# Rotating images by 180 degrees: SyncE's first load waits for a small memset on GpSimd

## The chip, the cores and the metric

The kernel runs on one core of one Trainium2 chip. The metric is the device time of one execution in microseconds (us). The kernel before took 122.02 us in the median of four runs (121.86 to 122.14).

## The reference

The input holds 32 x 3 images of 256 x 256 float32 numbers, 25.17 MB. The output has the same shape: each image turned by 180 degrees, which means that the 65,536 numbers of an image are written in reverse order.

```python
def reference(x):                       # x: (32, 3, 256, 256) float32
    return np.rot90(x, k=2, axes=(-2, -1)).astype(np.float32)
```

## The kernel before

The 96 images are taken in three groups of 32. In each group an image is cut into four rows of E = 16,384 numbers (64 KB), so a group is a tile of 128 partitions x 64 KB, which holds 8.39 MB. The tiles `A`, `Bt` and `Ct` hold the three groups, each in a buffer of its own, and all three groups stay in the on-chip memory: no load ever waits for a buffer. `T` is a scratch tile of 128 x 2,048 numbers (J = E / 8).

The work on one group has three steps.

- `load` brings rows from DRAM to a tile, in the order in which they stand there. One row of a load is one DMA packet for each partition.
- `inside` reverses the numbers of every row in place, on VectorE (DVE): for each of four pairs of blocks of 2,048 numbers it copies the upper block reversed to `T`, the lower block reversed to the upper place, and `T` to the lower place. These are 12 copies for each tile (line 52).
- `store` writes the tile back with the four rows of each image in reverse order (line 58). The reversal of the row order costs no instruction; it is in the address pattern.

Some transfers are cut in two. The load of `A` has a strip of the first `HEAD` = 512 numbers (2 KB of each row, 256 KB in all), issued by ScalarE (ACT); the other 62 KB of each row come in a second load, issued by SyncE (SP). The load of `Ct` is cut at its last 1,536 numbers (`TAIL`, 6 KB of each row). The store of `A` is cut after its first 128 numbers (`LEAD`, 512 bytes of each row). All transfers other than the strip are issued by SP, in this order: the rest of `A`, `Bt`, the body of `Ct`, the tail of `Ct`, the lead of `A`'s store, the rest of `A`'s store, the store of `Bt`, the store of `Ct`. The profile shows SP's queue as q1 and ACT's queue as q10. Both queues feed the same 16 DMA engines.

Two orders are written by hand. The DVE copies are kept in program order, and the large store of `A` waits until the body of `Ct` has landed, so that the tail of `Ct` is still on its way while that store is issued. The tile framework adds the remaining waits from the data that instructions share.

In the profile, lines 55 (loads), 52 (copies) and 58 (stores) carry the work; line 100 is the launch's preamble, with four small memsets on GpSimd (POOL), and line 111 its end.

Of the kernel before, what the change touches and what calls it, by code (L numbers as in the profile page):

```python
# [2 lines left out]

os.environ.setdefault("NEURON_RT_ULTRASERVER_MODE", "4")

# [4 lines left out]


@with_exitstack
def kernel(
    ctx: ExitStack,
    tc: tile.TileContext,
    x: bass.AP,
    out: bass.AP,
):

    nc = tc.nc
    P = 128

    B, C, H, W = x.shape
    L = H * W
    G = 32
    E = L // 4
    J = E // 8

    x4 = x.rearrange("b c h w -> (b c) (h w)").rearrange(
        "(g n) (s e) -> g (n s) e", n=G, s=4)
    o4 = out.rearrange("b c h w -> (b c) (h w)").rearrange(
        "(g n) (s e) -> g n s e", n=G, s=4)  # L40

    pool = ctx.enter_context(tc.tile_pool(name="slots", bufs=1))
    A = pool.tile([P, E], x.dtype, tag="A")
    Bt = pool.tile([P, E], x.dtype, tag="B")
    Ct = pool.tile([P, E], x.dtype, tag="C")
    T = pool.tile([P, J], x.dtype, tag="T")

    def back(t, lo, hi):
        return t[:, hi - 1:(lo - 1 if lo else None):-1]

    def copy(dst, src):
        tc.keep_in_program_order(nc.vector.tensor_copy(out=dst, in_=src))  # L52

    def load(t, g, lo, hi, queue=nc.sync):
        return queue.dma_start(out=t[:, lo:hi], in_=x4[g][:, lo:hi])  # L55

    def store(t, g, lo, hi):
        return nc.sync.dma_start(
            out=o4[g][:, ::-1, lo:hi], in_=t[:, lo:hi])

    def inside(t):
        for lo in range(0, E // 2, J):
            hi = E - lo - J
            copy(T[:, :], back(t, hi, hi + J))
            copy(t[:, hi:hi + J], back(t, lo, lo + J))
            copy(t[:, lo:lo + J], T[:, :])

    TAIL = 1536
    HEAD = 512
    load(A, 0, 0, HEAD, nc.scalar)  # L70
    load(A, 0, HEAD, E)
    load(Bt, 1, 0, E)
    body = load(Ct, 2, 0, E - TAIL)
    load(Ct, 2, E - TAIL, E)
    inside(A)
    LEAD = 128
    store(A, 0, 0, LEAD)
    first = store(A, 0, LEAD, E)
    tc.add_manual_dep(
        first.ins, body.ins.name,  # L80
        mybir.DependencyInfo(mybir.DependencyClass.Sync, mybir.DependencyReason.DATA),
        reason="the first store is queued while the last strip is on its way")
    for g, t in ((1, Bt), (2, Ct)):
        inside(t)
        store(t, g, 0, E)


# [1 line left out]
_INS = ['x']  # L89
_OUTS = [((32, 3, 256, 256), 'float32')]  # L90


# [23 lines left out]
```

## Time and profile before

| quantity | value |
|---|---|
| median of 4 runs | 122.02 us (121.86 to 122.14) |
| profiled execution, device time | 121.99 us |
| its span, first to last instruction | 120.2 us |
| DVE busy | 44.2 us (37%), 36 copies of 1.23 us |
| POOL busy | 0.2 us, 4 memsets of about 0.1 us |
| DMA, share of 16 engines | q1 97.0%, q10 0.6% |
| bytes | 25.17 MB read, 25.17 MB written, 419 GB/s over the span |
| issue of `A`'s rest (SP) and strip (ACT) | both at 0.73 us |
| landing after issue | rest 22.0 us, strip 22.1 us |

How to read it: the span is counted from the first instruction to the last; the device time of the profiled execution is 1.79 us longer. In a view by stretches of time, a DMA packet is counted whole, with its bytes and its duration, in the stretch in which it starts. So a short stretch in which 16 large packets start shows a DMA share far above 1, and the next stretch shows zero although the engines are at work. GB/s times the length of the stretch gives the bytes of the packets that started there, and the DMA share times the length times 16 gives the sum of their durations.

### The profile page before, as it was taken

What the parts mean: (1) busy time and instruction counts of PE and PEld (TensorE: products, weight loads), DVE (VectorE), ACT (ScalarE), POOL (GpSimd) and SP (SyncE); (2) the same over time, 40 slices, a digit from 0 to 9 for tenths busy, and PEclk for the clock granted to TensorE, in tenths of its full rate; (3) what the DMA queues carried; (4) which work ended last, traced back from release to release, by engine and by line L of the source; (5) the groups of instructions that cost most, each with busy time, mean ns of one, the idle gap of its engine ahead of it and who ended that gap; (6) DMA issues with size and microseconds to landing.
All of it is one profiled execution on the core that took longest, in us unless ns stands there. A gap on an engine that the chain in (4) does not pass through costs nothing.

```text
span 120.2 us, 97 instructions
## 1 busy us (share of the span) xinstructions
DVE 44.2 (37%) x36; POOL 0.2 (0%) x4
## 2 busy tenths in 40 slices
DVE  0000000499995099999049999500000000000000
POOL 0000000000000000000000000000000000000000
DMA  9888988898889779779499777988898889888990
GB/s 338 349 349 371 655 370 349 360 676 371 349 349 676 338 316 613 336 316 632 192 438 692 346 346 346 692 349 349 349 698 349 349 349 676 371 349 349 654 393 0
DMA packets 1296, 50.33 MB, mean 419 GB/s; under 512 B 144, under 2 KB 272, under 8 KB 528
## 3 DMA queue, kind: packets, MB, share of 16 engines
q1 hardware_dynamic: 1152, 50.07, 97.0%
q10 hardware_dynamic: 144, 0.26, 0.6%
HBM read 25.17 MB, written 25.17 MB: 419 GB/s over the span
## 4 chain that ended last, share of the span: by engine, by line
DMA 34%; DVE 25%; another core or an unknown queue 3%; issue 1%; SPq 0%; DVEq 0%
DMA Bt<-in_x_dram 34%; DVE T L52 8%; DVE Ct L52 8%; DVE Bt L52 8%; SPq L55 0%; DVEq L52 0%
## 5 line engine op out<-in xcount | busy, mean ns | idle before, releaser
L52 DVE COPY T<-A 128x2048 f32<-128x2048 f32 x4 | 4.9, 1227 | 22.8 <-DMA A<-in_x_dram 22.7
L52 DVE COPY T<-Bt 128x2048 f32<-128x2048 f32 x4 | 4.9, 1227 | 4.4 <-DMA Bt<-in_x_dram 4.3
L52 DVE COPY T<-Ct 128x2048 f32<-128x2048 f32 x4 | 4.9, 1227 | 4.4 <-DMA Ct<-in_x_dram 4.3
L52 DVE COPY A<-A 128x2048 f32<-128x2048 f32 x4 | 4.9, 1227 | 0.1
L52 DVE COPY Bt<-Bt 128x2048 f32<-128x2048 f32 x4 | 4.9, 1227 | 0.1
L52 DVE COPY Ct<-T 128x2048 f32<-128x2048 f32 x4 | 4.9, 1227 | 0.1
L52 DVE COPY Ct<-Ct 128x2048 f32<-128x2048 f32 x4 | 4.9, 1226 | 0.1
L52 DVE COPY A<-T 128x2048 f32<-128x2048 f32 x4 | 4.9, 1226 | 0.1
L52 DVE COPY Bt<-T 128x2048 f32<-128x2048 f32 x4 | 4.9, 1226 | 0.1
L100 POOL MEMSET const-bfloat16-1.0<- 128x1 bf16 x1 | 0.1, 102 | 0.0
L100 POOL MEMSET const-uint8-127<- 128x1 uint8 x1 | 0.1, 101 | 0.0
L100 POOL MEMSET const-float32-0.0<- 128x1 f32 x1 | 0.1, 99 | 0.2 <-issue 0.2
L100 POOL MEMSET const-float32-1.0<- 128x1 f32 x1 | 0.1, 98 | 0.0
## 6 DMA issues: line engine op xcount, KB each, us to landing
out_dram<-A SPq DMA_DIRECT2D x1, 8128.0 KB, 21.2
A<-in_x_dram SPq DMA_DIRECT2D x1, 7936.0 KB, 22.0
Ct<-in_x_dram SPq DMA_DIRECT2D x1, 7424.0 KB, 57.9
Ct<-in_x_dram SPq DMA_DIRECT2D x1, 768.0 KB, 59.3
A<-in_x_dram ACTq DMA_DIRECT2D x1, 256.0 KB, 22.1
out_dram<-A SPq DMA_DIRECT2D x1, 64.0 KB, 35.2
Bt<-in_x_dram SPq DMA_DIRECT2D x1, 40.9
out_dram<-Bt SPq DMA_DIRECT2D x1, 39.8
```

The costliest lines, as they stand in the source:

```text
L52: tc.keep_in_program_order(nc.vector.tensor_copy(out=dst, in_=src))
L100: nc = _bacc.Bacc("TRN2", target_bir_lowering=False, num_devices=1)
```

## The change

Before the loads, GpSimd gets a memset of the first 16 numbers of each row of `T` (`pause`). SP's load of the 62 KB of each row of `A` gets a manual dependency on that memset, with a semaphore. ACT's load of the strip has no such dependency. `load` now also keeps the loads in the program's order among themselves.

```diff
     def load(t, g, lo, hi, queue=nc.sync):
-        return queue.dma_start(out=t[:, lo:hi], in_=x4[g][:, lo:hi])
+        return tc.keep_in_program_order(
+            queue.dma_start(out=t[:, lo:hi], in_=x4[g][:, lo:hi]))
...
     HEAD = 512
+    pause = nc.gpsimd.memset(T[:, :16], 0.0)
     load(A, 0, 0, HEAD, nc.scalar)
-    load(A, 0, HEAD, E)
+    rest = load(A, 0, HEAD, E)
+    tc.add_manual_dep(
+        rest.ins, pause.ins.name,
+        mybir.DependencyInfo(mybir.DependencyClass.Sync, mybir.DependencyReason.DATA),
+        reason="the long packets are queued behind the strip")
     load(Bt, 1, 0, E)
```

## Prediction

> **What bounds the kernel now.** I read the page first: engine busy times, the DMA slices and the queues.
>
> ```profile
> DVE 44.2 (37%) x36; POOL 0.2 (0%) x4
> ...
> q1 hardware_dynamic: 1152, 50.07, 97.0%
> q10 hardware_dynamic: 144, 0.26, 0.6%
> ```
>
> The 16 DMA engines are busy 97.6% of 120.2 us, and DVE 37%. The 2.4% that is left is 2.9 us, and the windows below place most of it: the first packet starts after 1.70 us, and the last ones (started at 116.4 to 116.7, about 2.42 us long) end at about 119.1. So the kernel is bound by DMA from its first packet to its last, and this change can only move when the engines start and how evenly they run. The chain of waits names DVE for 25%, but it follows copies that the queue covers: the wait at the end is SP's, for the last store.
>
> ```profile
> SPq L111 <- DMA out_dram<-Ct: 38.6, 1, 38.6
> ```
>
> The last store was issued at 76.70 us and its packets began about 20 us later, behind other stores. DVE could finish many microseconds later at no cost.
>
> Next the timeline of the first 3 us.
>
> ```profile
> 0.33 0.10 POOL L100 MEMSET const-uint8-127<- 128x1 uint8 x1
> 0.73 0.39 SPq L55 DMA_DIRECT2D A<-in_x_dram  x1
> 0.73 0.38 ACTq L55 DMA_DIRECT2D A<-in_x_dram  x1
> 1.18 0.43 SPq L55 DMA_DIRECT2D Bt<-in_x_dram  x1
> 1.65 1.00 SPq L55 DMA_DIRECT2D Ct<-in_x_dram  x2
> ```
>
> SP's large load and ACT's strip are issued in the same moment. Which goes first is seen in the windows. Their columns are the stretch, its length, DVE and POOL busy time, clock, DMA share and GB/s; a packet counts where it starts.
>
> ```profile
> 1.70:2.10 0.40, 0.00 (x0) 0.00 (x0) 1.00 7.63 2540
> 2.10:4.60 2.50, 0.00 (x0) 0.00 (x0) 1.00 0.00 0
> 4.60:4.70 0.10, 0.00 (x0) 0.00 (x0) 1.00 0.05 20
> 4.70:5.30 0.60, 0.00 (x0) 0.00 (x0) 1.00 3.79 1638
> 5.30:5.40 0.10, 0.00 (x0) 0.00 (x0) 1.00 1.46 635
> 5.40:6.90 1.50, 0.00 (x0) 0.00 (x0) 1.00 0.00 0
> 6.90:7.80 0.90, 0.00 (x0) 0.00 (x0) 1.00 2.70 1165
> ```
>
> From 1.70 to 2.10 us, 2540 GB/s x 0.40 us = 1016 KB start, which is 16 x 63.5 KB: all 16 engines begin with a long packet and none with a 2 KB one. Their durations sum to 7.63 x 0.40 x 16 = 48.8 us, **3.05 us** each. From 4.60 to 4.70 one 2 KB packet starts (20 x 0.10 = 2 KB, 0.05 x 0.10 x 16 = **0.08 us**). From 4.60 to 5.40 together, 2 + 983 + 63.5 = 1049 KB start, which is 16 short and 16 long packets; from 6.90 to 7.80 it is 1049 KB again, lasting 2.70 x 0.90 x 16 = 38.9 us. Less 16 x 0.08 this is 37.6, or **2.35 us** for a long packet. So engines alternate, one packet of each queue, and the first long packet costs 0.70 us more than the second. Its excess is not equal on all engines: the first packets start within 0.40 us at most, but the second long ones start from 4.7 up to 5.3-5.4 us, a spread of 0.6 to 0.7.
>
> The lag stays. At the turn from loads to stores, the first long store packets start mostly in one 0.1 us stretch, and one engine follows late:
>
> ```profile
> 60.90:61.00 0.10, 0.00 (x0) 0.00 (x0) 1.00 11.14 4700
> 61.00:61.10 0.10, 0.00 (x0) 0.00 (x0) 1.00 6.13 2632
> 61.10:61.20 0.10, 0.00 (x0) 0.00 (x0) 1.00 0.07 20
> 61.20:61.30 0.10, 0.00 (x0) 0.00 (x0) 1.00 1.56 666
> ```
>
> **The change part by part.** The sum is made against the profiled execution, 121.99 us (span 120.2, and 1.79 around it), 0.03 us under the median of the runs.
>
> SP's wait. POOL's preamble rows end at 0.43 us, and SP and ACT begin at 0.73, so I let POOL begin there too. Its memset is 128x16; the nearest row is the 128x1 memset, 0.10 us. No row shows a POOL semaphore releasing an SP load; the nearest is DVE's copy, which ends at 26.47 (25.24 + 1.23) and releases SP's store at 26.50, 0.03 us. So SP issues at about 0.88 instead of 0.73: 0.15 us later. The upper bound is 0.5, as if the memset took as long as the preamble's four (0.20 us busy) and 0.3 went to the wait and its instruction. The lower bound is 0.1, the memset alone. I take 0.15 to 0.2, by the nearest rows. The three loads queued behind on SP (`Bt`, both parts of `Ct`) go back by as much, and for them it costs nothing: `A`'s packets keep the engines busy until about 22 us. DVE, which waits for `A` at 22.7, does not set the end.
>
> On the DMA engines 0.15 to 0.2 us is no loss if strip packets fill it. Per engine there are 8 x 0.08 = 0.67 us of strip (256 KB over 16 engines, 2 KB each). If the strip's first packets start where the long ones did, at 1.70 to 2.10, the long packets join at about 1.9 to 2.3, and from then each engine has work of both kinds, as before. Term: 0. With the cover gone it is +0.15 to +0.5.
>
> The first packet. Bytes and packets are the same, so the strip-first order saves nothing by itself. What can change is the 0.70 us excess. If it is a fixed start cost of an engine, the first 2 KB packet bears it and the term is 0. If it comes from 16 engines starting 62 KB reads together, it shrinks with the packet, by up to 0.70 x 60/62 = 0.68. A side below nothing (small first packets start worse) is not excluded by any row, but from 1.9 us on the long packets are there to fill a stall, so I bound it at +0.3. A fixed cost would hit all engines alike; the spread grew from at most 0.40 to 0.6-0.7, so some 0.2 to 0.3 is unequal, and I read that as contention. I take **-0.3**, near the unequal part.
>
> The rest. DVE's first copy gets one more wait, on a memset finished 21 us earlier: 0. SP's closing waits may get one more semaphore: 0 to +0.05, taken as 0. Program order among the loads is the order that they had: 0. POOL's extra memset has no one behind it but the end.
>
> Sum: 121.99 + 0 - 0.3 = 121.69, so **121.7 us**.
>
> The Trainium skill, "DMA: Bandwidth & Descriptors", section "Issuing engines are not separate DMA queues", speaks against a gain: transfers from different engines run on the same 16 DMA engines and a second issuer saves only issue time. The trace agrees that one set of engines serves both queues (they alternate above); by that rule alone the order is worth nothing and the time would be 122.0.
>
> The same page, section "Queues, rings and completion order", says that an engine drains a whole packet of typically 9 to 17 descriptors before it changes the queue. The rows above show a change after every single row of 2 KB. By the rule all eight strip rows of an engine would go in one turn; the sum is the same by both, since the engines stay busy.
>
> **The rivals.** *A wash, 122.0.* The excess is a fixed start cost and goes to the first 2 KB packet, and the wait hides behind the strip. For it: the bytes are unchanged, and the lag of the slowest engine shrinks by itself, from about 0.3 us behind most others at 61.2-61.3 to about 0.1 at the last packets (4588 GB/s in each of the stretches 116.4 to 116.5 and 116.5 to 116.6 is 459 KB, 7 packets of 64 KB each; the other two start from 116.6 to 116.7). Against it: the unequal excess. 0 to +0.2 gives 122.0 to 122.2.
>
> *The strip still isn't first, 122.3.* Both loads were issued at 0.73, yet all 16 engines took SP's packet first. If ACT's queue reaches the engines later by more than SP's new delay, the long packets go first again and everything starts later by the wait, with nothing in front. Place: the stretch from 1.7 to 2.1 us. Price: +0.15 to +0.5, 122.15 to 122.5, in the middle 122.3. It decides if ACT's first packets come over 0.2 us later than SP's did. No row excludes that, because ACT's packets had the long ones in front of them from 2.1 us. For it: 16 of 16 engines agree. Against: the two issues began and ended within 0.01 us of each other, so a small lead of SP's is enough to explain the order.
>
> **How the numbers follow.** About 0.2%, 0.24 us, is what a measurement of this kernel can tell from no change. Strip first with a smaller excess (121.7): 0.45. Wash (122.0): 0.27. Strip not first, or small packets that start worse (122.3): 0.28. The forecast's own range is 121.3 (excess gone) to 121.9; its weak end is a change within 0.2%, some 0.05 of its chance, and a long wait in the wash gives the slow side 0.02. So faster 0.40, same 0.30, slower 0.30. The range: 121.3 to 122.5 holds the cases; I set 121.25, for the runs' spread of 0.14 on either side, to 122.5.
>
> **What would show it.** Right: the timeline has SP's issue at 0.85 to 0.95 and ACT's at 0.73; the window 1.70 to 2.10 starts 2 KB packets; the strip lands earlier than the 22.1 us after its issue of now, and at most 0.2 us later than now the rest of `A`; the slowest engine's first long store packet starts before 61.2. Wrong: long packets of about 3.05 us still first, 0.2 us later; or the short first packets with an excess of 0.7 each, and the turn to the stores where it is now; or engines idle between the strip and the first long packet.

## The result and the profile after

The changed kernel takes 122.20 us in the median of 31 runs (122.01 to 122.58), the kernel before 122.02 us in 50 runs beside it. The ratio is 1.0016 (95% interval 1.001 to 1.0021): slower by 0.18 us, where -0.3 us was forecast. The profiled execution took 122.14 us with a span of 120.3 us, against 121.99 and 120.2 before.

The change does what it says. The timeline of the changed kernel from 0.6 us on (start, length, engine, line, operation):

```profile
0.73 0.11 POOL L71 MEMSET T<- 128x16 f32 x1 [0.29 <-POOLq L106]
0.73 0.36 ACTq L56 DMA_DIRECT2D A<-in_x_dram  x1
0.87 0.38 SPq L56 DMA_DIRECT2D A<-in_x_dram  x1
```

SP's large load is issued at 0.87 us in place of 0.73, 0.14 us later, and ACT's strip still at 0.73. The page of the changed kernel has the queues and, in its last column, the time from issue to landing:

```profile
q1 hardware_dynamic: 1152, 50.07, 96.5%
q10 hardware_dynamic: 144, 0.26, 0.9%
...
A<-in_x_dram SPq DMA_DIRECT2D x1, 7936.0 KB, 21.8
...
A<-in_x_dram ACTq DMA_DIRECT2D x1, 256.0 KB, 2.9
```

The strip lands 2.9 us after its issue, where it was 22.1 before: it goes first. The rest of `A` lands at 0.87 + 21.8 = 22.7 us, and before it was 0.73 + 22.0 = 22.7. So at the end of the first load nothing is won and nothing lost. The waits of DVE say the same for all three tiles (in total, times, longest):

```profile
DVE T L52 <- DMA A<-in_x_dram: 22.7, 1, 22.7
DVE T L52 <- DMA Ct<-in_x_dram: 4.3, 1, 4.3
DVE T L52 <- DMA Bt<-in_x_dram: 4.2, 1, 4.2
```

The kernel before had

```profile
DVE T L52 <- DMA A<-in_x_dram: 22.7, 1, 22.7
DVE T L52 <- DMA Bt<-in_x_dram: 4.3, 1, 4.3
DVE T L52 <- DMA Ct<-in_x_dram: 4.3, 1, 4.3
```

Where the start cost went is in the windows of the changed kernel (stretch, length, DVE, POOL, clock, DMA share, GB/s):

```profile
1.70:3.40 1.70, 0.00 (x0) 0.00 (x0) 1.00 2.06 752
3.40:5.05 1.65, 0.00 (x0) 0.00 (x0) 1.00 0.00 0
5.05:5.85 0.80, 0.00 (x0) 0.00 (x0) 1.00 2.95 1270
```

A KB is 1,000 bytes in these products. From 1.70 to 3.40 us, 752 x 1.70 = 1278 KB start: all 128 strip packets (262 KB) and the first long packet of each engine (1016 KB). Their durations are 2.06 x 1.70 x 16 = 56.0 us, 3.50 us for each engine. At the pace of the kernel before, eight strip packets of 0.084 us and a long one of 2.35 take 3.02. So an excess of 0.48 us is in the durations, most of it in the strips: by the packet records they last 0.129 us on average, against 0.084 before. The rest is spread wider: by the records, all packets of `A` together last 20.03 us on each engine, against 20.12 before, and a later mean start and gaps take up the difference. The first packet of `Bt`, which follows when the whole of `A` is done, starts on average over the 16 engines at 21.96 us, against 21.95 before. The 0.70 us were moved to other packets, not removed.

At the turn to the stores, one engine starts its first long store packet at 61.2 to 61.3 us, as before (one stretch of the changed kernel). The forecast had named that as a sign against it.

```profile
61.20:61.30 0.10, 0.00 (x0) 0.00 (x0) 1.00 1.52 655
```

A part of what was lost is at the other end. SP closes the kernel by waiting for the semaphores that the kernel used. The view of SP's instructions of the closing line in the stretch from 119.0 to 119.65 us (engine, operation, count: shortest, median and longest in ns, first and last start), first the kernel before in the stretch to 119.6, then the changed one:

```profile
L111 SPq DRAIN  x2: 7/7/7, 119.5 to 119.5; - x2
L111 SPq EVENT_SEMAPHORE  x1: 19317/19317/19317, 100.1 to 100.1; - x1
```

```profile
L117 SPq EVENT_SEMAPHORE  x2: 28/19372/38716, 80.8 to 119.5; - x2
L117 SPq DRAIN  x1: 7/7/7, 119.6 to 119.6; - x1
```

Before, one wait begins at 100.1 and lasts 19.3 us, until the last store has landed (119.4), and the drain follows at once. In the changed kernel a wait of 38.7 us ends with the last landing, and behind it stands another wait instruction of 28 ns at 119.5, with 37 ns to the drain. GpSimd's memset brought a semaphore of its own, and the list of closing waits became one instruction longer. All SP instructions of the closing line, the kernel before first:

```profile
L111 SPq EVENT_SEMAPHORE  x6: 17/28/19317, 77.3 to 120.1; - x6
L117 SPq EVENT_SEMAPHORE  x7: 17/28/38716, 77.2 to 120.3; - x7
```

The operands in the trace tell more. A wait instruction names at most two semaphores. Before, four waits and the drain cover nine, and the last of the four holds the last store's. With ten, there are five waits, and the last store's stands in the fourth. The fifth, the one of 28 ns, is for the store of `Bt` and for DVE, both met long before; GpSimd's own is on the drain. So the tenth semaphore shifted the grouping, and this put a wait behind the last landing. By the semaphore times of the traces, the last landing to the end of the span takes **0.79 us before and 0.86 after: 0.07 us more**, with no work to hide it.

### The profile page after: what moved, and what is told of

Same layout as the page of the kernel before. It is cut to its first block, busy times and chain, and to the rows that moved or that the text cites. A ratio compares the mean times of both kernels' runs of the same rounds, so it can differ in the third digit from the quotient of the medians.

```text
span 120.3 us, 100 instructions
## 1 busy us (share of the span) xinstructions
DVE 44.2 (37%) x36; POOL 0.3 (0%) x5
## 4 chain that ended last, share of the span: by engine, by line
DMA 34%; DVE 25%; another core or an unknown queue 4%; issue 1%; SPq 0%; POOLq 0%; DVEq 0%
DMA Bt<-in_x_dram 34%; DVE T L52 8%; DVE Bt L52 8%; DVE Ct L52 8%; SPq L56 0%; POOLq L117 0%; DVEq L52 0%; POOLq L106 0%
## 5 line engine op out<-in xcount | busy, mean ns | idle before, releaser
L52 DVE COPY T<-A 128x2048 f32<-128x2048 f32 x4 | 4.9, 1227 | 22.8 <-DMA A<-in_x_dram 22.7
## 6 DMA issues: line engine op xcount, KB each, us to landing
A<-in_x_dram SPq DMA_DIRECT2D x1, 7936.0 KB, 21.8
```

## The experiments

Theories. *Tail*: the added closing wait, 0.07 us, is the loss that can be pinned down, and the order at the start is worth nothing. *Order*: strip first is what costs. *GpSimd*: having GpSimd in the program costs it all. All ratios are to the kernel before, run beside it on the same chip.

**The changed kernel again**, no edit.

> The changed kernel once more, for a second profile beside the others. Known: 122.20 us, ratio 1.0016. Every theory expects 1.001 to 1.002. Tail theory: the last store lands within 0.1 us of where it does before, and the last landing to the end of the span takes 0.86 us against 0.79 before. Order theory: the last store itself lands 0.1 to 0.2 us later than before.

Measured 1.0023 (1.0009 to 1.0036), 0.86 us after the last landing. This profiled execution had a slow start on some engines (the strip landed as late as 4.18 us, the rest of `A` at 22.96), and was 122.49 us. Its last landing came at 119.84 us, 0.43 later than before, so the tail theory's sign (within 0.1 us) did not show. In the five profiles of the changed kernel the last landing is 0.07 to 0.43 us later than in the one profile of the kernel before, so by these profiles the closing wait is not all of the loss.

**SP waits for DVE's memset.**

```diff
-    pause = nc.gpsimd.memset(T[:, :16], 0.0)
+    pause = nc.vector.memset(T[:, :16], 0.0)
```

> The memset that SP waits for is on DVE instead of GpSimd: the strip still goes first, but no further engine's semaphore has to be waited for at the end. Tail theory (the added closing wait costs 0.07 us and something else 0.12): 122.13 us, ratio 1.0009, and 0.79 us from the last landing to the end. Order theory (strip first is what costs): 122.20, 1.0016. GpSimd theory (the cost is having GpSimd in the program at all): 122.02, 1.000.

Measured 1.000 (0.999 to 1.0009). SP issues at 0.90 us, the strip lands 3.0 us after its issue, and the closing line is back to one wait before the drain (stretch 119.0 to 119.65):

```profile
L117 SPq DRAIN  x2: 7/7/7, 119.5 to 119.5; - x2
L117 SPq EVENT_SEMAPHORE  x1: 19371/19371/19371, 100.1 to 100.1; - x1
```

0.79 us from the last landing to the end. DVE's semaphore was in the list already, so this memset adds none. A strip that goes first, with SP held back by 0.17 us, costs nothing that this run could see. That is against the order theory. The value is the one that the GpSimd theory gave; the tail theory's 1.0009 lies at the edge of the interval.

**GpSimd's memset alone**: the memset stays, the manual dependency goes.

```diff
     rest = load(A, 0, HEAD, E)
-    tc.add_manual_dep(rest.ins, pause.ins.name, ...)
```

> The GpSimd memset stays, SP's load does not wait for it, so long packets go first as before, and the end still waits for GpSimd's semaphore. Tail theory: 122.09 us, ratio 1.0006. Order theory: 122.02 to 122.05, 1.000. GpSimd theory: 122.20, 1.0016.

Measured 1.0009 (0.9996 to 1.0021), with long packets first, both loads issued at 0.73 and the longer end (stretch 119.0 to 119.8):

```profile
L113 SPq EVENT_SEMAPHORE  x2: 28/19334/38640, 81.0 to 119.6; - x2
L113 SPq DRAIN  x2: 7/7/7, 119.7 to 119.8; - x2
```

0.86 us after the last landing. The interval fits 1.0006 and cannot tell it from 1.000 or 1.0016; the trace's 0.07 us is the evidence.

**The strip ahead of the rest in SP's own queue.**

```diff
-    load(A, 0, 0, HEAD, nc.scalar)
+    load(A, 0, 0, HEAD)
```

> The kernel before with the strip issued by SP ahead of the rest of A: the strip is first in the one queue, nothing waits for a memset, and SP's large load is issued about 0.45 us later. Order theory: 122.20 us, 1.0016. Tail and GpSimd theories: 122.02, 1.000, or some 0.05 less if the start gets smoother.

Measured 1.0002 (0.9991 to 1.0014). The strip lands 2.8 us after its issue, and the end takes 0.79 us. Its windows are those of the changed kernel almost digit for digit:

```profile
1.70:3.40 1.70, 0.00 (x0) 0.00 (x0) 1.00 2.06 752
3.40:5.05 1.65, 0.00 (x0) 0.00 (x0) 1.00 0.00 0
5.05:5.85 0.80, 0.00 (x0) 0.00 (x0) 1.00 2.93 1270
```

So the start cost appears with strip-first whoever arranges it, and strip first is not what makes 0.18 us.

**A second comparison, with GpSimd beside DVE's wait.** The second kernel has both memsets, and SP waits for DVE's:

```diff
-    pause = nc.gpsimd.memset(T[:, :16], 0.0)
+    nc.gpsimd.memset(T[:, 16:32], 0.0)
+    pause = nc.vector.memset(T[:, :16], 0.0)
```

> The changed kernel a third time, as the measure for the three beside it. Known: 1.0016 and 1.0023 of the time before, 0.86 us from the last landing to the end. Expected again 1.001 to 1.003 by every theory.

> SP waits for DVE's memset, so the strip is first, and GpSimd does a memset of 16 other numbers of T that SP's load doesn't wait for. Closing theory (all of the loss that repeats is the added closing wait, 0.07 us): 0.86 us after the last landing, and 1.0005 to 1.001 of the time before. Release theory (the other 0.12 us come from SP's load being released by GpSimd instead of DVE): also 1.0005, and the changed kernel beside it stays at 1.0016 or more. Company theory (strip first together with a GpSimd memset costs 0.19): 1.0016.

Measured 1.0015 (1.0007 to 1.0024) for the changed kernel and 1.0008 (0.9999 to 1.0017) for the other; both take 0.86 us after the last landing. The closing wait goes with GpSimd's memset, whether a load waits for it or not. That 1.0008 is under the 1.0016 of the GpSimd theory, with an interval that just reaches it.

**How much delay the strip covers.** DVE's memset is 1,024 numbers in place of 16, once with SP's load alone waiting and once with both loads waiting:

```diff
-    pause = nc.vector.memset(T[:, :16], 0.0)
+    pause = nc.vector.memset(T[:, :1024], 0.0)
...
+    tc.add_manual_dep(strip.ins, pause.ins.name, ...)   # in the second kernel
```

> SP waits for a DVE memset of 1,024 numbers of each row, about 1.1 us, in place of 16, while ACT's strip is issued at once. Cover theory (strip packets fill SP's delay): SP issues at about 1.9 us, its packets come about 2.9, the strips end between 2.5 and 3.3 us: 0 to 0.4 us over the kernel before, 122.0 to 122.4. If the strip covered nothing, the whole delay of 1.2 us would show: 123.2.

> Both loads of A wait for the same 1.1 us DVE memset. A delay of the first packet by 1.2 us goes to the end undiminished: 123.2 us, if the DMA engines bound the kernel from first to last packet. Less than 0.8 us over the kernel before would mean that something in the middle takes up slack.

Measured 1.0101 (1.0085 to 1.0117), 123.16 us, and 1.0102 (1.0087 to 1.0117), 123.30 us. SP issues at 1.95 us in both, 1.22 later than before. For both loads the answer is plain: 1.22 us at the start give 1.24 at the end (1.02% of 122.01 us). For SP alone the cover theory expected at most 0.4 and was wrong by far. The windows of that kernel, with the packets at its start and its last packets:

```profile
1.70:2.90 1.20, 0.23 (x1) 0.00 (x0) 1.00 0.73 218
2.90:4.30 1.40, 0.00 (x0) 0.00 (x0) 1.00 2.09 726
4.30:5.70 1.40, 0.00 (x0) 0.00 (x0) 1.00 0.00 0
```

```profile
117.20:117.40 0.20, 0.00 (x0) 0.00 (x0) 1.00 3.79 1638
117.40:117.60 0.20, 0.00 (x0) 0.00 (x0) 1.00 6.82 2949
117.60:117.80 0.20, 0.00 (x0) 0.00 (x0) 1.00 0.76 328
117.80:118.00 0.20, 0.00 (x0) 0.00 (x0) 1.00 0.00 0
118.00:118.20 0.20, 0.00 (x0) 0.00 (x0) 1.00 0.76 328
```

All strip packets (218 x 1.20 = 262 KB) start before 2.90 us. The 16 long ones (726 x 1.40 = 1016 KB) start after it and last 2.09 x 1.40 x 16 / 16 = 2.93 us each: after a pause the long packets pay a start excess of 0.58 us once more. On average over the engines the first packet of `Bt` starts at 22.68 us, 0.73 later than before, so the mean engine got 0.49 of the 1.22 us back from the strip. At the last packets the mean start is 0.96 later, so half of that was gone again. And one engine starts its last packet at 118.0 to 118.2, some 0.6 us behind most of the other 15 (5 + 9 + 1 packets of 65.5 KB in the three stretches before), and the end is the slowest engine's. This execution, 123.50 us, was the slowest of four (the fastest 123.07); whether a late engine ate the cover in the other three too, no profile shows.

**A third comparison, and no strip at all.** The last kernel has one load of the whole 64 KB rows of `A` by SP:

```diff
-    load(A, 0, 0, HEAD, nc.scalar)
-    load(A, 0, HEAD, E)
+    load(A, 0, 0, E)
```

> The changed kernel beside the next two, to see whether anything is left over the added closing wait (0.07 us, 1.0006). Closing theory: 1.0006 to 1.001, and no more than 0.05 us above the DVE wait with a GpSimd memset beside it. Release theory (being released by GpSimd costs another 0.1 us): 1.0015 to 1.002, 0.1 us above it.

> SP waits for DVE's memset, GpSimd does one that nobody's load waits for. Both theories: 1.0006 to 1.001 of the time before, and 0.86 us from the last landing to the end.

> SP waits for DVE's memset, GpSimd has nothing to do: strip first without the added closing wait. Both theories: 1.000, between 0.9994 and 1.0006, and 0.79 us after the last landing.

> The kernel before without a strip: SP loads the whole 64 KB of each row of A, ACT issues nothing. If a start cost of about 0.7 us belongs to each engine's first packets whatever their size, and the order of bytes is worth nothing: 122.0 us, within 0.1. If the strip had any worth as the thing that runs first: slower than 122.15.

Measured: changed kernel 1.0019 (1.0001 to 1.0037), DVE's wait with GpSimd's memset 1.0008 (0.9999 to 1.0017), DVE's wait alone 1.0007 (0.9998 to 1.0016), which is above its range, and no strip 1.001 (1.0001 to 1.0019), 122.12 us, against 122.0 within 0.1 expected: just outside, and under the 122.15 that would have given the strip a worth. By its trace the last landing to the end takes 0.81 us there. Without a strip the first packets show the start cost by themselves (one stretch of that kernel):

```profile
1.70:2.60 0.90, 0.00 (x0) 0.00 (x0) 1.00 3.49 1165
```

1165 x 0.90 = 1049 KB are 16 rows of 64 KB, lasting 3.49 x 0.90 = 3.14 us each, 0.72 over the 2.42 of a later row. So the excess is 0.70 with 62 KB rows, 0.72 with 64 KB rows, 0.48 in the durations of the first nine packets (and more behind them) with 2 KB rows in front. It belongs to the start of the engines much more than to the size of the first packet. Nor do long reads pay for starting close together: in the kernel with the strip in SP's own queue, the first 16 rows of `Bt` start within 0.38 us of one another, and by the packet records each lasts 2.42 us.

**What is left over.** The changed kernel had come out at 1.0015 to 1.0023 in four comparisons, the one with DVE's wait and GpSimd's memset twice at 1.0008, although both have strip first and the longer end. The last four kernels looked for the difference: the first two as above, the third with a longer memset on GpSimd, the fourth with both loads waiting for GpSimd's 16 numbers.

```diff
-    pause = nc.gpsimd.memset(T[:, :16], 0.0)
+    pause = nc.gpsimd.memset(T[:, :64], 0.0)            # third kernel
...
+    tc.add_manual_dep(strip.ins, pause.ins.name, ...)   # fourth kernel
```

> The changed kernel, as the measure for the three beside it: 1.0015 to 1.002 of the time before. If the 0.1 us left over was chance, it comes out within 0.05 us of the DVE wait with a GpSimd memset.

> SP waits for DVE's memset, GpSimd does another: 1.0006 to 1.001, as twice before.

> The changed kernel with a memset of 64 numbers of each row in place of 16, so that GpSimd releases SP's load some 0.03 to 0.06 us later, about when DVE does. Moment theory (0.87 us is an unlucky moment, in which the long packets come between the strips and some engines fall behind): 1.0006 to 1.001. Releaser theory (GpSimd's release as such): 1.0015 or more.

> Strip and rest both wait for GpSimd's 16-number memset. ACT's and SP's loads are then issued together at about 0.87 us, and long packets go first as before. A start that is 0.14 us later and covered by nothing, and a closing wait of 0.07: 0.21 us, 1.0017, if the 0.1 us left over needs the strip to be first; 0.3 us, 1.0025, if it comes from GpSimd's release as such.

Measured 1.0017 (1.0007 to 1.0026), 1.0011 (1.0002 to 1.002), 1.0008 (0.9999 to 1.0017) and 1.0016 (1.0006 to 1.0025). In the third GpSimd releases SP at 0.91 us. In the fourth both loads are issued at 0.87 to 0.88, and 0.14 + 0.07 = 0.21 us was expected against 0.20 in the medians. That speaks against a cost of GpSimd's release as such, for which 1.0025 was expected, the upper end of the interval. It leaves the moment of release, but the intervals of 1.0017 and 1.0008 overlap, so it is not shown.

## Why the prediction was wrong

**What held.** DMA bounds the kernel from its first packet to its last: a start 1.22 us later ends 1.24 later. SP's new wait was put at 0.15 us with an issue at 0.88; it is 0.14, at 0.87. The strip does go first, so the rival in which it still isn't first falls, although its time of 122.3 is near. A delay of this size is mostly hidden behind the strip: the first packets of `Bt` start on average at 21.96 us, and in the other four profiles of the changed kernel at 22.00 to 22.07, against 21.95 to 21.96 in the three kernels that start with long packets at once. So the first load ends 0.01 to 0.12 us later. One reading was off and bears on nothing: the packets of the last store begin 22.8 us after its issue, not about 20.

**The step that failed** is the term of the first packet, -0.3 us. It took the unequal part of the 0.70 us excess for contention among long packets, which would shrink with their size. The runs show a start cost that comes with a small first packet too: the strip's packets last 0.129 us in place of 0.084, more is lost behind them, and nothing is won by the time `A` is done (21.96 against 21.95 us). The kernel without a strip has 0.72, and long packets after a pause pay 0.58 again. The wash rival had this right. An unequal excess was no proof of contention; a start cost that differs from engine to engine looks the same.

**The term that was mis-sized** is the closing wait, "0 to +0.05, taken as 0". It measures 0.07 us in each of the eleven profiles with a GpSimd memset of the kernel's own (0.86 us after the last landing) against the six others that keep the strip (0.79, the kernel before among them). The forecast named the added semaphore and left out that a wait may come to stand behind the last landing, where nothing hides it.

**The cover was overrated.** The prediction counted the 0.67 us of strip on each engine as cover. With a delay of 1.22 us the mean engine had 0.49 of it, and the time next to nothing that four executions of each could tell (1.0101 against 1.0102 without any cover, each to within 0.0016).

**The sum that the runs give.** The start: 0, or up to 0.09 us (1.000 and 1.0007 with DVE's wait). The end: +0.07. Together +0.07 to +0.16 of the 0.18 measured. The two are worked out from different kernels, so this is an estimate. The five comparisons of the changed kernel lie at 1.0015 to 1.0023, the three of its neighbour with DVE's wait and GpSimd's memset at 1.0008 to 1.0011. **What stays open** is this difference of about 0.1 us (1.0017 against 1.0008 in the middle). By the medians it is smaller, 0.14 to 0.22 us over the kernel before against 0.09 to 0.14; single long executions such as one of 123.22 us raise the ratios. In some profiles of the changed kernel late engines are seen at the last packets, as in these windows, the kernel before first and then the third profile of the changed kernel:

```profile
116.30:116.60 0.30, 0.00 (x0) 0.00 (x0) 1.00 7.07 3058
116.60:116.75 0.15, 0.00 (x0) 0.00 (x0) 1.00 2.02 874
116.75:116.90 0.15, 0.00 (x0) 0.00 (x0) 1.00 0.00 0
```

```profile
116.30:116.60 0.30, 0.00 (x0) 0.00 (x0) 1.00 7.07 3058
116.60:116.75 0.15, 0.00 (x0) 0.00 (x0) 1.00 0.00 0
116.75:116.90 0.15, 0.00 (x0) 0.00 (x0) 1.00 2.02 874
```

3058 x 0.30 = 917 KB are 14 packets, and two more start 0.15 us or more behind them. In the profile before all 16 start before 116.7. A measure of it is how far the last landing lies behind the mean start of the 16 last packets. By the packet records this is 2.87 to 2.91 us in the four kernels in which long packets go first beside a strip, 2.93 to 3.08 in the five profiles of the changed kernel, 2.91 to 2.96 in the three of its neighbour, and 3.00 and 3.05 with DVE's wait alone. So the engines end less evenly when the strip goes first, by about 0.1 us in the changed kernel, which is of the size that is missing. But the kernel without a strip has 3.13, DVE's wait has it without the time to match, and one profile of each run doesn't make a mean. Whether SP's release at 0.87 us leaves more of them than at 0.90 was not settled.

**The Trainium skill** said in "DMA: Bandwidth & Descriptors", section "Issuing engines are not separate DMA queues", that a second issuing engine only saves issue time. The runs agree: the strip from ACT with SP waiting for DVE, from SP's own queue, or behind the long packets gives the same time within 0.1%, and this rule should have had more weight than the hope for a smaller excess. Its section "Queues, rings and completion order" has an engine drain several descriptors before it changes the queue. The kernel before shows a change after every row; in the changed kernel, where the strip has a lead of 0.14 us, all 128 strip packets have started by 3.22 us and the first long packet ends at 5.13, so no strip row waited for a long one. So here both orders occur, and the time tells them apart by 0.1% at most.

No version came out faster than the kernel before.

## What to carry to other kernels

When transfers bound a kernel from the first packet to the last, don't expect time from a new order of its first packets (here none of the orders won any); look for what makes the first packet earlier or the last landing cheaper. An instruction on an engine that the kernel did not use yet brings a semaphore to the closing list, and this can leave one more wait behind the last landing, where nothing hides it: borrow an engine whose semaphore is waited for already (here DVE). Don't count a few small packets as full cover for a delay: the large ones behind them may pay the start a second time (0.58 us in one profile here), and the slowest engine sets the end.

## What the runs showed that was not expected

The start excess of the 16 engines, 0.70 us with 62 KB rows and 0.72 with 64 KB rows, did not go away with 2 KB rows in front (0.48 in the first nine packets, and `A` done no sooner), and it comes back, 0.58 us, when the strip has run out before the long packets come. Of two loads issued within 0.01 us, SP's went first on all 16 engines, and a lead of 0.14 us for ACT's was enough to turn that round. A longer list of closing waits costs 0.07 us although the semaphore that made it longer had been met since the first microsecond: what counts is which waits stand behind the one for the last landing.
